# Readout matrices beside the injection, late modulation and scan at fewer steps a chunk

## Chip, core and metric

One core of a Trainium2 chip runs the whole program. The time is device time in microseconds from one launch to its end; the median of several runs is given, and one run more is recorded by the hardware profiler. Five engines work from queues of their own, each strictly in its queue's order: TensorE (PE; its weight loads are shown as PEld), VectorE (DVE), ScalarE (ACT), GpSimd (POOL) and SyncE (SP, which here only issues DMA transfers).

## What is computed

One layer of a generator for 512 latent tokens of width 2048 and 256 context tokens. Cut to the parts that the change touches:

```python
mod_lat = jax.nn.silu(c) @ w_mod[l] + b_mod[l]
sh1, sc1, g1, sh2, sc2, g2 = jnp.split(mod_lat[:, None, :], N_MOD, axis=-1)
h = modulate(x, norm1_w[l], sh1, sc1)
z = h @ w_in[l]
y_a = s5_branch(z[..., :S5_WIDTH], ...)      # bidirectional diagonal state space, 64 groups
y_b = pool_branch(z[..., S5_WIDTH:S5_WIDTH + POOL_WIDTH], ...)
x = x + g1 * merge_branches(z, y_a, y_b, proj_a[l], proj_b[l], w_out[l])
x = x + g2 * peer_ffn(modulate(x, norm2_w[l], sh2, sc2), ...)
# merge_branches: (sigmoid(gate_a) * (y_a @ proj_a) + sigmoid(gate_b) * (y_b @ proj_b)) @ w_out
```

## The kernel before

Everything is float32. A product takes three matmuls: high half by high half, high by low, low by high. `wload` brings a weight chunk of 512 KB to `wraw` by SP, ScalarE copies its high half `whi` (L125), and VectorE (in the expert stage also GpSimd) subtracts for the low half `wlo` (L126). A chunk feeds 24 matmuls of 512 columns in the stages before the experts.

The stages in the order of the program: modulation and normalisation; the state space's input `zs` (`psz`); the pooling inputs and four blocks of the first gate (`psz`, then `psg`), beside which the injection runs; the window products with the matrix `wm` (`psp`, L732) and the pooling products (`psy`); the gates with the projection `proj_b` (`psg`, `psp`, eight blocks of six chunks, then four of four); the readout of the state space (`psr`); the merge (`w_glu`, `proj_a`); the output projection `w_out` (`pso`); then the experts, about two thirds of the time.

Small work that no big product needs at once runs in *lanes*: generators, of which `tick`, called once for each weight chunk, takes a number of steps given by the lane's rate. In this kernel:

- `s5_inject` (rate 2.5) turns `zs` through the loaded matrices `m1` into the states' inputs `B` (`psb`, L663); its loads and stores are issued by GpSimd.
- `s5_scan` (rate 4) runs the recurrence over `B` on VectorE, four operations a step (L678 to L681), 94 steps and 8 steps of reordering.
- `s5_toeplitz` and `s5_m3` (rate 0.7) make the readout's matrices. The first adds two diagonals (`gdiag`) and stores them eight times into `td`, and copies the rest in DRAM. The second makes 32 groups of six GpSimd operations each (L616 to L621) in the tile `m3`, of which there is one, and stores each group to `m3d` by SP (L622). The next group's first write to `m3` (L616) waits until the store is done.
- `mod_late` (rate 3.4) makes the last four quarters of the modulation, each in four blocks of 512 columns. A step loads 256 KB of `w_mod` (`lw`, by SP) and accumulates on VectorE (`lacc`, L819); after the 16 steps of a block one TensorE product sums over the partitions (`psl`, L824), VectorE adds the bias (`lrow`), and GpSimd stores the row to `modd`.

The tile framework gives each tile buffers of its pool, reuses the space of a closed pool, adds the waits that follow from both, and sets each engine's order by a timeline of its own; `high_priority` moves instructions ahead in it. So the order in the code isn't that of the queues. The tiles of the pool `zp` (`wm` and the window products) and of the scan take space that the injection's pools have left.

## Time and profile before

| | us |
|---|---|
| three runs, median (lowest, highest) | 3934.92 (3920.32, 3938.32) |
| profiled execution, device time | 3923.52 |
| its span, first to last instruction | 3921.8 |
| TensorE busy, VectorE busy | 3686.4, 2732.1 |
| GpSimd busy, ScalarE busy | 1834.7, 1178.3 |

In the profile, "busy" of TensorE holds matmuls that overlap in the pipeline: one of 0.39 us is followed by the next after 0.23. A table of stages shows busy times in stretches that I chose by the first and last rows of each stage. A list of waits says which engine's line sat idle for which other, in total, how often, and at most. In the list of single instructions, the bracket at the end of a row is idle time ahead of it and what ended that. SPq is SP's queue; a duration there is that of the issue, and a transfer lands later.

### The profile page before, as it was taken

To read this page: it belongs to the slowest core of one execution; us is meant where nothing else is said; L and a number is where in the kernel's file an instruction comes from. 1 tells how busy PE (TensorE), PEld (TensorE's weight loads), DVE (VectorE), ACT (ScalarE), POOL (GpSimd) and SP (SyncE) were. 2 spreads that over 40 slices of the span, in tenths; PEclk is the share of its full clock that TensorE was granted. 3 is DMA by queue.
4 is the path that set the end of the run, shared out by engine and by line. 5 is a ranking of instruction groups with operands and counts; after the bars stand their busy time and mean duration, and the time that the engine had idled before them with its cause. 6 is when DMAs were issued, how large, how long until landed. Compare 5 with 4: busy or idle time off the path is not lost. (4 is left out here: it accounts for less than half of the span.)

```text
span 3921.8 us, 49308 instructions
## 1 busy us (share of the span) xinstructions
PE 3686.4 (94%) x18841; PEld 3128.2 (80%) x18841; DVE 2732.1 (70%) x3331; ACT 1178.3 (30%) x1752; POOL 1834.7 (47%) x997
## 2 busy tenths in 40 slices
PE   5999998879899989899999999999999999999997
PEld 2478876657777868799999999999877878878886
DVE  4364369997473268999999999965666665666564
ACT  3223331112232232233333333333332333333232
POOL 0043115553223223355555655555565776676652
PEclk8999999999999999999999999999999999999999
DMA  8635658879876422378878878788887988888773
GB/s 263 213 118 182 213 165 231 225 218 289 245 235 199 135 75 91 105 248 285 299 282 300 301 286 300 278 300 296 320 301 258 321 298 286 304 298 298 273 278 120
DMA packets 456381, 954.40 MB, mean 243 GB/s; under 512 B 104720, under 2 KB 248464, under 8 KB 421072
## 3 DMA queue, kind: packets, MB, share of 16 engines
q1 hardware_dynamic: 380320, 584.58, 46.6%
q0 software_dynamic: 46464, 301.03, 21.0%
q10 hardware_dynamic: 29360, 65.64, 4.5%
q8 instruction: 147, 2.41, 0.2%
q14 instruction: 90, 0.74, 0.1%
HBM read 859.88 MB, written 94.93 MB: 243 GB/s over the span
## 5 line engine op out<-in xcount | busy, mean ns | idle before, releaser
L125 ACT CAST whi<-wraw 128x1024 fp32r<-128x1024 f32 x712 | 746.4, 1050 | 1724.9 <-PE psU L111 307.3
L126 POOL TENSOR_TENSOR wlo<-wraw,whi 128x1024 fp32r<-128x1024 f32 x284 | 792.5, 2791 | 803.6 <-ACT whi L125 591.6
L126 DVE TENSOR_TENSOR wlo<-wraw,whi 128x1024 fp32r<-128x1024 f32 x428 | 621.2, 1451 | 560.1 <-ACT whi L125 309.4
L112 PE MATMUL psU<-h2Th,wlo 128*128 128x384 f32 x2048 | 696.8, 340 | 42.5 <-DVE wlo L126 26.0
L110 PE MATMUL psU<-h2Th,whi 128*128 128x384 f32 x2048 | 702.0, 343 | 5.2 <-ACT whi L125 5.1
L111 PE MATMUL psU<-h2Tl,whi 128*128 128x384 f32 x2048 | 694.3, 339 | 0.0
L111 PE MATMUL psV<-wlo,ah 128*128 128x512 f32 x1536 | 607.0, 395 | 12.9 <-POOL wlo L126 7.1
L112 PE MATMUL psV<-whi,al 128*128 128x512 f32 x1536 | 605.9, 394 | 0.0
L110 PE MATMUL psV<-whi,ah 128*128 128x512 f32 x1536 | 556.1, 395 | 4.3 <-DVE ffn L1231 4.3
L112 PEld LDWEIGHTS psU<-h2Th,wlo 128*128 128x128 f32 x2048 | 388.8, 190 | 50.9 <-DVE wlo L126 19.3
L1096 DVE SCALAR_TENSOR_TENSOR row<-row,h 128x2048 f32<-128x2048 f32 x128 | 352.3, 2752 | 81.8 <-DMA row<-in_u,eid 81.7
L110 PEld LDWEIGHTS psU<-h2Th,whi 128*128 128x128 f32 x2048 | 388.6, 190 | 7.3 <-ACT whi L125 7.1
L111 PEld LDWEIGHTS psU<-h2Tl,whi 128*128 128x128 f32 x2048 | 389.0, 190 | 0.0
L1089 DVE SCALAR_TENSOR_TENSOR ffn<-row,w,ffn 128x2048 f32<-128x2048 f32 x127 | 351.3, 2766 | 18.0 <-DMA row<-in_v,eid 17.9
L111 PEld LDWEIGHTS psV<-wlo,ah 128*128 128x128 f32 x1536 | 290.1, 189 | 85.5 <-POOL wlo L126 11.7
L1081 POOL DMA_INDIRECT row<-in_u,eid x128 | 221.4, 1730 | 269.4 <-ACT w L1097 132.5
L110 PEld LDWEIGHTS psV<-whi,ah 128*128 128x128 f32 x1536 | 289.7, 189 | 71.1 <-issue 4.7
L112 PEld LDWEIGHTS psV<-whi,al 128*128 128x128 f32 x1536 | 289.5, 189 | 67.0
L1081 POOL DMA_INDIRECT row<-in_v,eid x128 | 277.0, 2164 | 20.0 <-issue 9.2
L819 DVE SCALAR_TENSOR_TENSOR lacc<-lw,sil,lacc 128x512 f32<-128x512 f32 x240 | 213.7, 891 | 58.6 <-DMA lw<-in_w_mod 56.5
L112 PE MATMUL psg<-hhi,wlo 128*128 128x512 f32 x512 | 203.1, 401 | 25.9 <-DVE wlo L126 25.8
L1144 DVE TENSOR_TENSOR oh<-io,iT 128x512 bf16<-128x512 bf16 x192 | 211.6, 1141 | 6.3 <-PE psd L1152 6.2
(349 smaller groups left out, 5567.4 us busy)
## 6 DMA issues: line engine op xcount, KB each, us to landing
wraw<-in_uT SPq DMA_DIRECT2D x256, 512.0 KB
wraw<-in_v SPq DMA_DIRECT2D x256, 512.0 KB
lw<-in_w_mod SPq DMA_DIRECT2D x256, 256.0 KB
wraw<-in_w_in SPq DMA_DIRECT2D x96, 512.0 KB
wmod<-in_w_mod SPq DMA_DIRECT2D x48, 512.0 KB
sd<-sev ACTq DMA_DIRECT2D x64, 384.0 KB
gds<-ast ACTq DMA_DIRECT2D x12, 2048.0 KB
sr<-sd SPq DMA_DIRECT2D x32, 768.0 KB
```

Source lines behind the costliest of these rows:

```text
L110: mm(ps, a.hi, b.hi, start=start, stop=False)
L111: mm(ps, a.hi, b.lo, start=False, stop=False)
L112: mm(ps, a.lo, b.hi, start=False, stop=stop)
L125: nc.scalar.copy(hi, raw)
L126: ins = (eng or nc.vector).tensor_tensor(lo, raw, hi.bitcast(F32), op=OP.subtract)
L819: nc.vector.scalar_tensor_tensor(acc, w, self.sil[:, k, 0:1], acc, op0=OP.mult, op1=OP.add)
L1081: nc.gpsimd.indirect_dma_start(out=r, out_offset=None, in_=I[tab], in_offset=bass.IndirectOffsetOnAxis(ap=eid[:, k:k + 1], axis=0))
L1089: V.scalar_tensor_tensor(acc, v, w, acc, op0=OP.mult, op1=OP.add)
L1096: V.scalar_tensor_tensor(u, u, 1.0, h2, op0=OP.mult, op1=OP.mult, accum_out=w[:, 0:1])
L1144: V.tensor_tensor(oh[:, q], self.io4, iT[:, q, ts].unsqueeze(2).broadcast_to([P, NT, P]), op=OP.is_equal)
```

## The change

The two generators of readout matrices become one lane of rate 1.3, the matrices first, which starts with the injection and is emptied before the window products; both use the one pool `m3`, the diagonals in four rounds of 256 columns, in the tile of the matrices, in place of two of 512. `par2` is loaded for eight groups of the state space at a time in place of four. The injection's `m1` comes in halves of 256 KB, in buffers of half the size. The scan's lane goes from 4 to 2 steps a chunk. The late modulation's goes from 3.4 to 2.4, holds three of the four quarters, has two accumulators, and sums a block six steps into the next one; the last quarter becomes a second lane (rate 1.3) beside merge and output projection, with a pool of its own on the left side of SBUF. The readout ticks the lanes twice in each of its eight blocks.

The diff, cut:

```diff
@@ -192,6 +192,8 @@
         self.tail()
+        self.drain(self.lane_g2)
+        self.es_g2.close()
         self.peer()
...
@@ -374,22 +376,26 @@
         s5 = self.es()
+        es_m3 = self.es()
+        lane_m = self.lane(1.3, [self.s5_m3(es_m3), self.s5_toeplitz(es_m3)])
         lane_i = self.lane(2.5, [self.s5_inject(s5)])
...
         with self.es() as s6:
-            yb, lane_s = self.pool_branch(s6, es_b, hlat, s5, lane_i)
-            lane_m = self.lane(0.7, [self.s5_toeplitz(), self.s5_m3()])
-            lane = self.lane(3.4, [self.mod_late()])
+            yb, lane_s = self.pool_branch(s6, es_b, hlat, s5, lane_i, lane_m, es_m3)
+            lane = self.lane(2.4, [self.mod_late("late", "right", ((0, 2), (2, 4), (1, 3)))])
             self.gates(hlat, yb)
         es_h.close()
         self.drain(lane_s)
-        self.drain(lane_m)
         self.check("gates")
+        self.es_g2 = self.es()
+        late2 = self.mod_late("late2", "left", ((3, 5),))
+        next(late2)
         with self.es() as s7:
             gt = self.s5_readout(s7)
             self.drain(lane)
             es_b.close()
+            self.lane_g2 = self.lane(1.3, [late2])
             es_m = self.es()
             m = self.merge(s7, es_m, gt)
         self.m, self.es_m = m, es_m
...
-    def s5_toeplitz(self):
...
-        with self.es() as es:
-            sp = es.enter_context(self.tc.tile_pool(name="toep", bufs=1, side="right"))
-            for hf in range(2):
-                cs = slice(hf * 512, hf * 512 + 512)
-                gf = sp.tile([H, 2, 512], F32, tag="gdiag", name=self.nm("gdiag"))
-                nc.sync.dma_start(gf[:, 0], self.gd[112:128, 0, cs])
-                nc.sync.dma_start(gf[:, 1], self.gd[0:16, 1, cs])
-                nc.gpsimd.tensor_tensor(gf[:, 0], gf[:, 0], gf[:, 1], op=OP.add)
-                for t in range(Q):
-                    nc.sync.dma_start(self.td[t * H:(t + 1) * H, t, cs], gf[:, 0])
...
+    def s5_toeplitz(self, es):
+
+        nc, sp = self.nc, self.m3p
+        for q4 in range(4):
+            cs = slice(q4 * 256, q4 * 256 + 256)
+            gf = sp.tile([H, 2, 256], F32, tag="m3", name=self.nm("gdiag"))
+            nc.sync.dma_start(gf[:, 0], self.gd[112:128, 0, cs])
+            nc.sync.dma_start(gf[:, 1], self.gd[0:16, 1, cs])
+            nc.gpsimd.tensor_tensor(gf[:, 0], gf[:, 0], gf[:, 1], op=OP.add)
             for t in range(Q):
+                nc.sync.dma_start(self.td[t * H:(t + 1) * H, t, cs], gf[:, 0])
+            yield
+        for t in range(Q):
+            if t:
+                nc.sync.dma_start(self.td[0:t * H, t, :], self.gd[(Q - 1 - t) * H:(Q - 1) * H, 0, :])
...
+            if t % 2:
+                yield
...
-    def s5_m3(self):
+    def s5_m3(self, es):
...
-        with self.es() as es:
-            sp = es.enter_context(self.tc.tile_pool(name="m3", bufs=1, side="right"))
+        sp = self.m3p = es.enter_context(self.tc.tile_pool(name="m3", bufs=1, side="right"))
+        if True:
...
-                if gq * GM % 4 == 0:
-                    par = sp.tile([P, 2, H, 4], F32, tag="par2", name=self.nm("par2"))
-                    nc.sync.dma_start(par, self.I["s5bc"][gq * GM // GB][:, 2:4, :, gq * GM % GB:gq * GM % GB + 4])
...
+                if gq * GM % GB == 0:
+                    par = sp.tile([P, 2, H, GB], F32, tag="par2", name=self.nm("par2"))
+                    nc.sync.dma_start(par, self.I["s5bc"][gq * GM // GB][:, 2:4])
...
@@ -652,15 +658,15 @@
-                m1 = mp.tile([P, 4, 2, P], F32, tag="m1", name=self.nm("m1"))
-                nc.gpsimd.dma_start(m1.rearrange("p g r d -> p (g r d)"), self.m1d[gb, :, g4 * 1024:(g4 + 1) * 1024])
-                if g4 == 0 and i + 1 < NGB:
-                    nxt = chunks(order[i + 1])
                 for g2 in range(2):
+                    m1 = mp.tile([P, 2, 2, P], F32, tag="m1", name=self.nm("m1"))
+                    nc.gpsimd.dma_start(m1.rearrange("p g r d -> p (g r d)"), self.m1d[gb, :, g4 * 1024 + g2 * 512:g4 * 1024 + g2 * 512 + 512])
+                    if g4 == 0 and g2 == 0 and i + 1 < NGB:
+                        nxt = chunks(order[i + 1])
                     ps = self.psT.tile([P, 512], F32, tag="tr", name=self.nm("psb"))
...
@@ -691,7 +697,7 @@
-    def pool_branch(self, es, es_b, hlat, s5, lane_i):
+    def pool_branch(self, es, es_b, hlat, s5, lane_i, lane_m, es_m3):
...
@@ -718,8 +724,10 @@
             self.drain(lane_i)
             s5.close()
+            self.drain(lane_m)
+            es_m3.close()
             self.scp = es_b.enter_context(pool(name="scan", bufs=2, side="right"))
-            lane_s = self.lane(4, [self.s5_scan()])
+            lane_s = self.lane(2, [self.s5_scan()])
...
@@ -801,16 +809,32 @@
-    def mod_late(self):
...
-        nc, es = self.nc, self.es()
-        lp = es.enter_context(self.tc.tile_pool(name="late", bufs=4, side="right"))
+    def mod_late(self, name, side, parts):
...
+        nc = self.nc
+        es = self.es() if side == "right" else self.es_g2
+        lp = es.enter_context(self.tc.tile_pool(name=name, bufs=4 if side == "right" else 2, side=side))
-        for q, blk in ((0, 2), (2, 4), (1, 3), (3, 5)):
+        pend = None
+
+        def close(acc, q, n, c0):
+            row = lp.tile([1, N], F32, tag="lrow", name=self.nm("lrow"), bufs=1)
+            nc.gpsimd.dma_start(row, self.I["b_mod"][0:1, c0:c0 + N])
+            ps = self.psT.tile([P, 512], F32, tag="tr", name=self.nm("psl"))
+            nc.tensor.matmul(ps[0:1, :], self.ones[:, 0:1], acc, start=True, stop=True)
+            nc.vector.tensor_tensor(row, row, ps[0:1, :], op=OP.add)
+            nc.gpsimd.dma_start(self.modd[:, q * D + n * N:q * D + (n + 1) * N], row)
+
+        if side == "left":
+            yield
+        for q, blk in parts:
             for n in range(D // N):
                 c0 = blk * D + n * N
-                acc = lp.tile([P, N], F32, tag="lacc", name=self.nm("lacc"), bufs=1)
+                acc = lp.tile([P, N], F32, tag="lacc", name=self.nm("lacc"), bufs=2)
                 for k in range(KT):
+                    if k == 6 and pend is not None:
+                        close(*pend)
+                        pend = None
                     w = lp.tile([P, N], F32, tag="lw", name=self.nm("lw"))
...
                     yield
-                row = lp.tile([1, 2, N], F32, tag="lrow", name=self.nm("lrow"), bufs=1)
-                nc.gpsimd.dma_start(row[:, 1], self.I["b_mod"][0:1, c0:c0 + N])
-                ps = self.psT.tile([P, 512], F32, tag="tr", name=self.nm("psl"))
-                nc.tensor.matmul(ps[0:1, :], self.ones[:, 0:1], acc, start=True, stop=True)
-                nc.vector.tensor_tensor(row[:, 0], row[:, 1], ps[0:1, :], op=OP.add)
-                nc.gpsimd.dma_start(self.modd[:, q * D + n * N:q * D + (n + 1) * N], row[:, 0])
-                yield
-        es.close()
+                pend = acc, q, n, c0
+        for _ in range(6):
+            yield
+        close(*pend)
+        yield
+        if side == "right":
+            es.close()
...
@@ -860,6 +883,8 @@
                     nc.sync.dma_start(dsk, I["s5_d"][0:1, ch].broadcast_to([NCL, P]))
+                self.tick()
+                self.tick()
```

What that does to the queues, at three places. The first is GpSimd's queue where the four early gate blocks end (`sad` are their stores, `m` with 128x1024 or 128x512 the injection's loads, the other `m` and `m3t` a group of readout matrices). Before:

```order
L656 DMA m_535_3291<-m1d 128x1024
L656 DMA m_541_3339<-m1d 128x1024
L781 DMA sad<-sg_3984 128x512
L781 DMA sad<-sg_3987 128x512
L822 DMA lrow_4611<-in_b_mod 1x16x32
L584 TENSOR_TENSOR gdiag_4275<-gdiag_4275 16x512
L584 TENSOR_TENSOR gdiag_4287<-gdiag_4287 16x512
L608 TENSOR_SCALAR npar_4384<-par_698_4382 128x64
L616 TENSOR_TENSOR m_700_4386<-pm_4380,par_698_4382 128x256
L617 TENSOR_TENSOR m3t_4387<-pm_4380,par_698_4382 128x256
```

and now:

```order
L622 TENSOR_TENSOR m_594_3517<-pm_3051,par_556_3298 128x256
L625 TENSOR_TENSOR m_594_3517<-pm_3051,npar_3300 128x256
L789 DMA sad<-sg_4409 128x512
L624 TENSOR_TENSOR m_594_3517<-m_594_3517,m3t_3518 128x256
L789 DMA sad<-sg_4412 128x512
L663 DMA m_571_3380<-m1d 128x512
L663 DMA m_578_3408<-m1d 128x512
L626 TENSOR_TENSOR m3t_3518<-pm_3051,par_556_3298 128x256
L652 DMA ud<-U_3386 128x8x64
L627 TENSOR_TENSOR m_594_3517<-m_594_3517,m3t_3518 128x256
L663 DMA m_585_3457<-m1d 128x512
L614 TENSOR_SCALAR npar_3580<-par_604_3578 128x128
```

The last two `sad` stores stood behind every load of the injection, with the groups behind them and beside the gates; now they stand in the sixteenth of the 32 groups (tiles `m_419` to `m_688` in the order of the rows), and eight loads of the injection are still behind them.

The second is SP's queue around the load of `wm`. Before:

```order
L741 DMA wraw_4116<-in_pool_w 128x2x256
L741 DMA wraw_4144<-in_pool_w 128x2x256
L124 DMA wraw_4175<-in_w_in 128x4x256
L726 DMA wm<-in_wm 128x512
L124 DMA wraw_4242<-in_w_in 128x4x256
L124 DMA wraw_4347<-in_w_in 128x4x256
L124 DMA wraw_4431<-in_w_in 128x4x256
L815 DMA lw_4209<-in_w_mod 128x512
```

and now:

```order
L628 DMA m3d<-m_688_4096 128x512
L586 DMA gdiag_4135<-gd 16x256
L587 DMA gdiag_4135<-gd 16x256
L590 DMA td<-gdiag_4135 16x256 x8
L586 DMA gdiag_4177<-gd 16x256
...
L590 DMA td<-gdiag_4231 16x256 x8
L734 DMA wm<-in_wm 128x512
L124 DMA wraw_4653<-in_w_in 128x4x256
...
L839 DMA lw_4623<-in_w_mod 128x512
```

The load of `wm` followed the pooling weights and the next gate chunk; now it follows the last `m3d` stores and the four rounds of diagonals, and the gates' next weight chunks and the late modulation's first loads follow it. TensorE's first product with `wm` is row 1539 of its order before and now, right behind the last product of the injection.

The third is SP's queue at the readout's first loads (`rU`, `rT`, `rm`, `rd`). Before:

```order
L854 DMA rU_7944<-ud 128x512
L622 DMA m3d<-m_1273_6948 128x512
L815 DMA lw_7248<-in_w_mod 128x512
L856 DMA rT_7946<-td 128x8x128
L858 DMA rm_1451_7948<-m3d 128x4x512
L124 DMA wraw_7413<-in_w_in 128x4x256
L815 DMA lw_7251<-in_w_mod 128x512
L862 DMA rd_7952<-in_s_d 64x128
L854 DMA rU_7996<-ud 128x512
```

and now:

```order
L124 DMA wraw_8527<-in_w_glu 128x4x256
L839 DMA lw_8366<-in_w_mod 128x512
...
L877 DMA rU_7790<-ud 128x512
L879 DMA rT_7792<-td 128x8x128
L881 DMA rm_1392_7794<-m3d 128x4x512
L885 DMA rd_7798<-in_s_d 64x128
L877 DMA rU_7857<-ud 128x512
...
L885 DMA rd_7865<-in_s_d 64x128
L839 DMA lw_8146<-in_w_mod 128x512
```

The first two sets stood among weight chunks of the gates; now they stand behind all of these and behind the first chunks of `w_glu`, with accumulation loads ahead of them and after them. On VectorE 171 accumulation steps stand between the first and the last low half of the gates, before 199; 42 stand beside the readout's first products, before 10.

## Rows read from the trace of the kernel before

**Rows 1.** Table of stages.

```profile
core 0: us, PE busy (x) PEld busy (x) DVE busy (x) ACT busy (x) POOL busy (x), PEclk, DMA share, GB/s
378.00:527.40 149.40, 146.13 (x811) 125.35 (x809) 49.06 (x69) 53.09 (x115) 26.90 (x40) 1.00 0.65 200
527.40:989.00 461.60, 406.30 (x1672) 311.65 (x1672) 406.83 (x702) 95.92 (x115) 205.09 (x257) 0.96 0.81 234
989.00:1063.00 74.00, 60.25 (x461) 55.65 (x461) 25.49 (x34) 14.28 (x18) 20.06 (x11) 0.91 0.88 242
1063.00:1200.00 137.00, 132.29 (x569) 103.88 (x568) 99.67 (x119) 43.31 (x56) 43.61 (x29) 1.00 0.73 233
1200.00:1384.00 184.00, 180.56 (x773) 144.87 (x771) 58.86 (x59) 46.32 (x65) 49.65 (x45) 1.00 0.48 158
```

**Rows 2.** Single TensorE instructions: start us, us, engine, line, tiles, how many, idle before.

```profile
527.38 7.38 PE L732 MATMUL psp<-wm,us 128*128 128x128 f32 x64 [2.96 <-DMA wm<-in_wm]
...
549.16 0.39 PE L110 MATMUL psg<-hhi,whi 128*128 128x512 f32 x1
...
551.20 0.39 PE L110 MATMUL psg<-hhi,whi 128*128 128x512 f32 x1
...
980.62 1.02 PE L824 MATMUL psl<-lacc,ones 128*1 128x512 f32 x2
```

**Rows 3.** Waits of TensorE in the gates: us in total, times, longest.

```profile
PE psg L112 <- DVE wlo L126: 25.8, 15, 5.6
PE psp L112 <- DVE wlo L126: 22.1, 10, 4.0
PE psl L824 <- DVE lacc L819: 7.2, 4, 3.3
```

**Rows 4.** VectorE's groups in the gates (busy us, mean ns), then ns min/median/max of two.

```profile
L819 DVE SCALAR_TENSOR_TENSOR lacc<-lw,sil,lacc 128x512 f32<-128x512 f32 x185 | 166.4, 899 | 41.3 <-DMA lw<-in_w_mod 40.1
L126 DVE TENSOR_TENSOR wlo<-wraw,whi 128x1024 fp32r<-128x1024 f32 x65 | 84.1, 1295 | 5.5 <-ACT whi L125 4.8 <-PE psg L112 0.6
L678 DVE TENSOR_TENSOR sa<-ar,B 128x128 f32<-128x128 f32 x92 | 39.9, 434 | 1.1
...
L678 DVE TENSOR_TENSOR sa<-ar,B x94: 271/292/2406, 525.3 to 876.7; 128x128 f32<-128x128 f32 x94
...
L819 DVE SCALAR_TENSOR_TENSOR lacc<-lw,sil,lacc x240: 732/752/2549, 552.1 to 1142.6; 128x512 f32<-128x512 f32 x120
```

**Rows 5.** Single GpSimd instructions, end of preparation and last gate store.

```profile
378.15 0.86 POOL L636 DMA_DIRECT2D R<-zs  x1 [18.48 <-PE pg L563]
...
521.58 0.55 POOL L781 DMA_DIRECT2D sad<-sg  x1 [0.46 <-ACT sg L780]
```

**Rows 6.** Single GpSimd instructions, one diagonal round and a matrix group.

```profile
566.61 1.79 POOL L584 TENSOR_TENSOR gdiag<-gdiag 16x512 f32<-16x512 f32 x1 [9.65 <-DMA lw<-in_w_mod]
...
690.59 0.62 POOL L616 TENSOR_TENSOR m<-pm,par 128x256 f32<-128x256 f32 x1
...
693.62 0.72 POOL L621 TENSOR_TENSOR m<-m,m3t 128x256 f32<-128x256 f32 x1
...
698.61 0.78 POOL L616 TENSOR_TENSOR m<-pm,par 128x256 f32<-128x256 f32 x1 [3.23 <-DMA m3d<-m]
```

**Rows 7.** Single issues in SP's queue: start us, us, line, transfer, how many.

```profile
524.49 0.34 SPq L726 DMA_DIRECT2D wm<-in_wm  x1
...
557.84 3.28 SPq L586 DMA_DIRECT2D td<-gdiag  x7
...
562.70 0.32 SPq L582 DMA_DIRECT2D gdiag<-gd  x1
...
695.34 0.38 SPq L622 DMA_DIRECT2D m3d<-m  x1
```

**Rows 8.** Table of stages, the fullest slice for DMA.

```profile
900.00:950.00 50.00, 45.81 (x197) 36.65 (x198) 35.25 (x42) 10.39 (x12) 19.23 (x26) 1.00 0.99 315
```

**Rows 9.** Readout's first loads: ns min/median/max, first and last start us.

```profile
L854 SPq DMA_DIRECT2D rU<-ud x8: 326/357/576, 898.7 to 1043.4; - x8
```

More of the change, by code (lines that the diff above doesn't have):

```diff
@@ L573, in s5_prep @@
             yield
[L574 to L594 removed]
+    def s5_toeplitz(self, es):
[6 more added lines that the diff above has]
+            nc.gpsimd.tensor_tensor(gf[:, 0], gf[:, 0], gf[:, 1], op=OP.add)
+            for t in range(Q):
+                nc.sync.dma_start(self.td[t * H:(t + 1) * H, t, cs], gf[:, 0])
[3 more added lines that the diff above has]
+                nc.sync.dma_start(self.td[0:t * H, t, :], self.gd[(Q - 1 - t) * H:(Q - 1) * H, 0, :])
+            if t < Q - 1:
+                nc.sync.dma_start(self.td[(t + 1) * H:P, t, :], self.gd[H:(Q - t) * H, 1, :])
+            if t % 2:
+                yield
+    def s5_m3(self, es):
         nc, Gp = self.nc, self.nc.gpsimd
         GM = 2
[L598 to L599 removed]
+        sp = self.m3p = es.enter_context(self.tc.tile_pool(name="m3", bufs=1, side="right"))
+        if True:
             for gq in range(G // GM):
@@ L603, in s5_m3 @@
                     nc.sync.dma_start(pm, self.pmd[gq * GM // 16])
-                if gq * GM % 4 == 0:
-                    par = sp.tile([P, 2, H, 4], F32, tag="par2", name=self.nm("par2"))
-                    nc.sync.dma_start(par, self.I["s5bc"][gq * GM // GB][:, 2:4, :, gq * GM % GB:gq * GM % GB + 4])
-                    npar = sp.tile([P, H, 4], F32, tag="npar", name=self.nm("npar"))
+                if gq * GM % GB == 0:
+                    par = sp.tile([P, 2, H, GB], F32, tag="par2", name=self.nm("par2"))
+                    nc.sync.dma_start(par, self.I["s5bc"][gq * GM // GB][:, 2:4])
+                    npar = sp.tile([P, H, GB], F32, tag="npar", name=self.nm("npar"))
                     Gp.tensor_scalar(npar, par[:, 0], -1.0, None, op0=OP.mult)
                 shp = [P, Q, H, GM]
-                gl = slice(gq * GM % 4, gq * GM % 4 + GM)
+                gl = slice(gq * GM % GB, gq * GM % GB + GM)
                 gp = slice(gq * GM % 16, gq * GM % 16 + GM)
@@ L662, in s5_inject @@
                         for ri in range(2):
-                            nc.tensor.matmul(ps[:, (2 * j + ri) * NCH:(2 * j + ri + 1) * NCH], m1[:, g2 * 2 + j, ri, :],
+                            nc.tensor.matmul(ps[:, (2 * j + ri) * NCH:(2 * j + ri + 1) * NCH], m1[:, j, ri, :],
                                              U[:, g4 * 4 + g2 * 2 + j, :], start=True, stop=True)
```

6 lines of the change are left out of this document (removed).

## The prediction, made before the changed kernel was run

> **What bounds the kernel now.** I read the table of stages first, then the waits, then single rows. In the table [rows 1] the injection (378 to 527.4) leaves TensorE no gap: it is busy 146.1 of 149.4 us, while GpSimd has 26.9 us of work. The gates (527.4 to 989) are the stage that loses time: VectorE is busy 406.8 of 461.6 us. What TensorE has to do there is countable: 64 weight chunks (8 x (4 + 2) + 4 x 4) of 24 matmuls are 1536 matmuls, and an undisturbed one starts 0.227 us after the other (nine steps in 2.04 us [rows 2]), so 348 us; 48 more for the pooling products are 11, the window products 7.4, and twelve modulation sums of 1.0 us are 12 [rows 2]. That is a floor of 378 us, and 461.6 - 378 = 84 us are lost. The waits say to whom: to VectorE's low halves of the weights, 25.8 and 22.1 us, and to the modulation's accumulator, 7.2 us [rows 3].
>
> VectorE's groups in that stage say why [rows 4]: 185 accumulation steps of 899 ns (and 41 us of waiting, nearly all for their weights), 65 low halves, and 92 scan steps of four operations. The durations are swollen: the accumulation's median is 752 ns, the first scan operation's 292 against a mean of 434, with single ones up to 2406 ns. In the same stretch GpSimd is busy 205 us [rows 1], most of it with the 32 readout-matrix groups.
>
> **The change, part by part.**
>
> *(a) Readout matrices beside the injection: a wait of TensorE.* In GpSimd's new order the 32 groups of six operations stand between the injection's loads; the last pair of `sad` stores of the four early gate blocks stands within the 16th group, so 16 whole groups are behind it. On SP's queue the load of `wm` stands behind all 32 `m3d` stores and four diagonal rounds, and in TensorE's order the first product with `wm` has the same 1539 rows ahead of it as before. Engines take their rows in order, so TensorE can do nothing else in that time, and the scan, the gates' weight loads and the late modulation wait behind the same load. When `wm` lands is the sum of a chain:
>
> - The groups can't start before 378.15, where GpSimd leaves the preparation [rows 5]. The last `sad` issue is at 521.58 in the trace [rows 5] and waits for TensorE's gate blocks. The first 16 groups need 8.2 to 9.5 us each: 7.2 from below, plus `par` loads and 0.55 to 0.9 us for each DMA issue in between, of which there are 16 more because `m1` comes in halves. 16 x 9 from 382 is 526. I take 530, with 518 (no delay of the gate blocks) and 560 (the queues hold one another up) as bounds.
> - A group lasts from one L616 to the next: 690.59 to 698.61, 8.0 us [rows 6]. In it five operations end at 694.34; SP issues the store at 695.34 [rows 7], a microsecond late because it was busy with other loads; and the buffer, of which there is one, is free at 698.61, 3.3 us after the issue. Without the delay it is 7.0. I take 7.2 (6.9 to 8.0): 16 x 7.2 = 115 us, and 5 us for the rest of the 16th group and its store.
> - Four loads of `par` must land before their `npar`: some 1.5 us each beyond the store's wait, 6 us (4 to 12), estimated from the 3.3 us of a store.
> - A diagonal round: load at 562.70 [rows 7], its add at 566.61 [rows 6], 3.9 us; an add of half the size, 1 us (1.8 for the full one); eight stores of 0.47, 3.8 us (seven in 3.28 [rows 7]); the buffer back at most 1.6 us later (the first round's stores end at 561.12, the next load is at 562.70). That is 10 us, and there are four in place of two, one after the other because they share the matrices' one buffer: 40 us (38 to 46).
> - `wm` itself: issue at 524.49 [rows 7], first product at 527.38 [rows 2], 3 us.
>
> Sum: 530 + 5 + 115 + 6 + 40 + 3 = 699, against 527.4 before: **+172 us**, with 151 and 227 from the bounds. It can't come out below zero: 16 groups at the 4.4 us that six operations alone take (3.75 and one more of 0.62 [rows 6]) put the landing past 620.
>
> *(b) The gates without the groups, and slower lanes.* By the order 171 accumulation steps lie in the gates, before 199. VectorE loses 28 x 0.9 = 25 us of them; if the rest falls to the medians, 25 more there, some 38 in the scan (145 us for the four operations to 93 x 1.15) and 5 in the low halves. 407 becomes about 315, below TensorE's floor, and all 84 lost microseconds could come back. I take **-50** (20 to 85): in the new order the steps come in bunches, four to six of them in 32 of the 64 chunks and none in 24. A chunk with five and one scan step is 1.2 + 5 x 0.75 + 1.15 = 6.1 us of VectorE against 5.45 of TensorE, and it loads 5 x 256 + 512 KB, 330 GB/s, more than the 315 of the fullest stretch here [rows 8]. The wait of 7.2 us for the accumulator goes: there are two now, and the sum is put off by six steps.
>
> The Trainium skill, "SBUF — State Buffer", section "Who interferes with whom", says that a VectorE instruction with two SBUF inputs and a GpSimd instruction that reads SBUF shut each other out for a whole instruction. The trace agrees in direction (single operations of 2406 ns against a median of 292 [rows 4]); the page says nothing of the loads. By it alone the gates would fall to their floor, which is rival 5.
>
> *(c) The readout starts later.* Before, its first loads go out from 898.7 [rows 9], 90 us ahead of the first product. Now they stand behind the last gate chunk, their tiles wait for the last gate's `sad` store, and 42 accumulation steps stand among the readout's VectorE work in place of 10. Exposed: some 5 us for the store (3.3 for an `m3d` store, with its issue and the sigmoid ahead of it) and 7 for a set of 2 MB at 290 GB/s; then 32 x 256 KB = 8 MB more are 28 us, of which the stretch has room for about half (it moves 242 GB/s now [rows 1]). 12 + 14 = 26; I take **+22** (8 to 35).
>
> *(d) At nothing:* the last quarter's 64 steps (48 us at the median) beside merge and output projection, where VectorE is busy 99.7 of 137 and 58.9 of 184 us [rows 1]. If that cover failed, TensorE, idle 4.7 and 3.4 us there, would lose some 10 us. The quarter's `modd` stores on GpSimd hold `x1d` stores back by a few microseconds, and nobody waits for those. The scan at two steps a chunk takes 51 of 64 chunks and ends some 70 us before the readout.
>
> **Sum:** 172 - 50 + 22 = +144. The profiled execution took 3923.5 us (span 3921.8), near the fastest of the three runs shown (3920.3 to 3938.3, median 3934.9). 3923.5 + 144 = 4067.5, so **4068 us**.
>
> **The rivals.**
> 1. *The matrices do fit beside the injection* (faster). Then (a) is zero: 3923.5 - 50 + 22 = 3896, or 3861 with 85 from the gates. For it: GpSimd is idle over 120 us there. Against it: 32 groups and four rounds would have to be done in 149 us, 3.4 us a group, and six operations alone take 4.4. That figure decides it.
> 2. *A short wait, and gates at their floor.* The stores come back as fast as the diagonal's, 1.6 us, so a group is 5.4, and the early half keeps pace (518): 518 + 4 + 16 x 5.4 + 4 + 36 + 3 = 651, +124; with -85 and +8 the time is 3970. Against it: the store of the matrices at 698.61, with 3.3 us.
> 3. *The queues hold one another up.* GpSimd's next group waits for a store; SP issues it behind a weight load, which waits for VectorE and so for TensorE, which waits for an injection load behind the group on GpSimd. At the upper bounds (a) is +227, and with -35 and +22 the time is 4137. For it: SP's microsecond of delay. Against it: only the injection's loads tie TensorE to this circle.
> 4. *The change doesn't do what it says:* the gates stay bound by loads and bunches, -5: 3923.5 + 172 - 5 + 22 = 4112.
> 5. *The gates fall to their floor.* With the groups gone every VectorE operation takes its median, 315 us in all, and the loads keep up with the bunches: 3923.5 + 172 - 85 + 22 = 4032. For it: the swollen means; against it: the 330 GB/s of a bunch.
>
> [...]
>
> **Chances and range.** Forecast 0.57, rival 1 0.03, rival 2 0.10, rival 3 0.12, rival 4 0.06, rival 5 0.12. The range goes from 3995, which leaves out rivals 1 and 2, to 4135, which takes in rivals 4 and 5 and about half of rival 3. A measurement of this kernel can tell about 0.5% (20 us) from no change: faster 0.03, within 0.02 (the lower end of rival 2), slower 0.95.
>
> **What would show it.** Right: TensorE idle in one piece of 150 to 200 us that ends with the first `wm` product near 700, its wait put down to the load of `wm`; GpSimd's groups about 7.2 us apart in it; from there to the readout some 410 us; scan operations near 290 ns. Wrong: `wm` at 560 or earlier, groups closer than 5 us, or gates as long as 455 us.

## The result, and the profile after

The changed kernel takes 4025.7 us (median of four runs, 4021.95 to 4036.49) against 3928.0 before: a ratio of 1.0242, 95% interval 1.0213 to 1.0270. It is slower by 98 us where +144 was forecast; the profiled execution's span went from 3921.8 to 4020.2. The table of stages of the kernel after (columns as in [rows 1]; the stretches again by the first and last rows of each stage):

```profile
core 0: us, PE busy (x) PEld busy (x) DVE busy (x) ACT busy (x) POOL busy (x), PEclk, DMA share, GB/s
374.00:545.00 171.00, 158.18 (x807) 134.95 (x805) 51.31 (x61) 52.05 (x113) 119.14 (x171) 0.91 0.67 207
545.00:658.70 113.70, 0.00 (x0) 0.03 (x1) 3.54 (x14) 0.54 (x2) 57.64 (x90) 0.50 0.14 45
658.70:1044.00 385.30, 380.69 (x1666) 306.12 (x1666) 309.49 (x665) 95.40 (x114) 22.16 (x41) 0.99 0.69 222
1044.00:1063.30 19.30, 0.29 (x3) 0.07 (x2) 8.45 (x12) 2.91 (x4) 1.62 (x3) 0.63 1.05 328
...
1138.00:1288.00 150.00, 141.75 (x630) 113.77 (x629) 95.14 (x108) 45.36 (x57) 43.95 (x27) 0.98 0.66 205
```

The second row is new: 113.7 us in which TensorE does nothing, VectorE next to nothing, and GpSimd half of the time. The third is the gates, 461.6 us in [rows 1] and 385.3 now, with TensorE busy nearly throughout. The fourth is a hole of 19 us ahead of the readout, with the DMA engines full. The waits of TensorE (us in total, times, longest) name all three, the first three lines from the gates with the stretch ahead of them, the last two from the readout:

```profile
PE psp L740 <- DMA wm<-in_wm: 114.0, 1, 114.0
PE psg L112 <- DVE wlo L126: 2.9, 2, 1.6
PE psp L112 <- DVE wlo L126: 1.7, 2, 1.3
...
PE psr L896 <- DMA rT<-td: 22.7, 4, 19.0
PE psr L897 <- DMA rm<-m3d: 7.4, 4, 3.8
```

The 25.8 and 22.1 us of [rows 3] have become 2.9 and 1.7. VectorE's groups in the gates (busy us, mean ns of one, idle ahead), which answer [rows 4]:

```profile
L843 DVE SCALAR_TENSOR_TENSOR lacc<-lw,sil,lacc 128x512 f32<-128x512 f32 x158 | 118.1, 748 | 35.6 <-DMA lw<-in_w_mod 34.7
L126 DVE TENSOR_TENSOR wlo<-wraw,whi 128x1024 fp32r<-128x1024 f32 x65 | 79.2, 1220 | 26.7 <-PE psg L112 16.7 <-issue 7.2 <-PE psp L112 2.4
L684 DVE TENSOR_TENSOR sa<-ar,B 128x128 f32<-128x128 f32 x91 | 26.2, 288 | 1.5
```

The accumulation's mean is 748 ns (899 before), the scan's first operation 288 (434): both are at the median of before.

A ledger of both profiled executions, by the first and last TensorE rows of each stage:

| us | before | after | difference | forecast |
|---|---|---|---|---|
| start of the program to first `wm` product | 527.4 | 658.7 | +131.3 | +172 |
| to the last gate product | 461.3 | 385.2 | -76.1 | -50 |
| to the first readout product | 0.4 | 19.4 | +19.0 | +22 for these two |
| to the first product of the output projection | 211.8 | 224.8 | +13.0 | |
| to the experts (first `psU`) | 392.4 | 399.9 | +7.5 | 0 |
| experts | 2328.5 | 2332.2 | +3.7 | 0 |

### The profile page after: what moved, and what is told of

Read it like the earlier page. It is cut to its first block, busy times and chain, and to the rows that moved or that the text cites. A ratio compares the mean times of both kernels' runs of the same rounds, so it can differ in the third digit from the quotient of the medians.

```text
span 4020.2 us, 49345 instructions
## 1 busy us (share of the span) xinstructions
PE 3689.3 (92%) x18841; PEld 3141.6 (78%) x18841; DVE 2677.5 (67%) x3331; ACT 1175.9 (29%) x1752; POOL 1809.7 (45%) x1007
## 5 line engine op out<-in xcount | busy, mean ns | idle before, releaser
L126 DVE TENSOR_TENSOR wlo<-wraw,whi 128x1024 fp32r<-128x1024 f32 x428 | 610.0, 1426 | 548.4 <-ACT whi L125 283.1
L843 DVE SCALAR_TENSOR_TENSOR lacc<-lw,sil,lacc 128x512 f32<-128x512 f32 x240 | 199.2, 831 | 96.8 <-DMA lw<-in_w_mod 95.0
L1169 DVE TENSOR_TENSOR oh<-io,iT 128x512 bf16<-128x512 bf16 x192 | 220.9, 1190 | 9.7 <-PE psd L1177 9.7
L1171 DVE TENSOR_TENSOR R<-oh,wb 128x1536 bf16<-128x1536 bf16 x96 | 203.0, 2115 | 1.7
```

What stands on the lines that cost most here:

```text
L126: ins = (eng or nc.vector).tensor_tensor(lo, raw, hi.bitcast(F32), op=OP.subtract)
L843: nc.vector.scalar_tensor_tensor(acc, w, self.sil[:, k, 0:1], acc, op0=OP.mult, op1=OP.add)
L1169: V.tensor_tensor(oh[:, q], self.io4, iT[:, q, ts].unsqueeze(2).broadcast_to([P, NT, P]), op=OP.is_equal)
L1171: V.tensor_tensor(R, oh[:, 1].unsqueeze(1).broadcast_to([P, 3, NT, P]), wb[:, :, ts].unsqueeze(3).broadcast_to([P, 3, NT, P]), op=OP.mult)
```

## Experiments

The theory is that these are separate effects: the emptying of the matrices' lane costs the wait for `wm`; the missing groups, through GpSimd's operations, give the gates' gain; and the second late pool and the slower lanes cost the readout. The rivals put the gates' gain down to the slower lanes or to less traffic, and the readout's loss to its loads' place in the queue. All times below are medians, and each ratio is to the kernel before as run beside it; stages come from the profiled executions, of which there is one for each kernel, and they scatter: with the same code ahead of `wm`, its first product came between 653.3 and 661.9 us in the changed kernel and experiments 2, 4 and 5, and the experts, which no edit touches, took 2325.8 to 2338.2 us.

**1. The slower lanes alone.** The matrices stay beside the gates:

```diff
-        lane_m = self.lane(1.3, [self.s5_m3(es_m3), self.s5_toeplitz(es_m3)])
...
+            lane_m = self.lane(0.7, [self.s5_toeplitz(), self.s5_m3()])
             lane = self.lane(2.4, [self.mod_late("late", "right", ((0, 2), (2, 4), (1, 3)))])
```

> The changed kernel with the readout matrices back beside the gates, in pools of their own at 0.7 steps a chunk as before; everything else of the change stays (scan at 2, late modulation at 2.4 with the fourth quarter later, halves of m1, ticks in the readout). Theory: the wait for wm is gone (first wm product near 527), the stage from there to the last gate product takes about 440 us (461.6 before, 385 after), since VectorE has 27 accumulation steps fewer but GpSimd's groups still swell its operations (scan operations near 430 ns); the readout still starts about 19 us after the last gate product, and 22 to 32 us are lost there. Time 3923 - 20 + 28, about 3930. Rival A, the gates' gain of the change is all from the slower lanes: 390 us in the gates, scan operations near 290 ns, time near 3880. Rival B, it is all from the missing groups: 460 us, time near 3950.

3975.7 us, ratio 1.0095 (1.0059 to 1.0131). The gates take 453.7 us, only 8 less than before, and the readout begins 21.2 us late and takes 225.0. VectorE's and GpSimd's groups in the gates:

```profile
L841 DVE SCALAR_TENSOR_TENSOR lacc<-lw,sil,lacc 128x512 f32<-128x512 f32 x158 | 137.4, 869 | 37.2 <-DMA lw<-in_w_mod 35.7
L684 DVE TENSOR_TENSOR sa<-ar,B 128x128 f32<-128x128 f32 x92 | 38.1, 414 | 1.6
L627 POOL TENSOR_TENSOR m<-m,m3t 128x256 f32<-128x256 f32 x32 | 27.4, 855 | 2.1
```

With as few steps as in the kernel after, the means are nearly those of [rows 4]. The theory expected 20 us from the lanes; it is 8, nearer to rival B's nothing. Rival A falls. The first `wm` product came at 538.95, 12 us later than before, which nothing in the theory provided for (experiment 9). The time is 45 us above the 3930 expected: besides these 12 and the 12 missing in the gates, the hole and the readout cost 34 us in place of 28, and the stages from the output projection on are 14 longer than before.

**2. The matrices alone**, old lanes and old late modulation:

```diff
-            lane = self.lane(2.4, [self.mod_late("late", "right", ((0, 2), (2, 4), (1, 3)))])
+            lane = self.lane(3.4, [self.mod_late()])
...
-            lane_s = self.lane(2, [self.s5_scan()])
+            lane_s = self.lane(4, [self.s5_scan()])
...
```

> The kernel before with only the matrices moved beside the injection and emptied before the window products (and m1 in halves); scan at 4, late modulation at 3.4 steps with all four quarters, no ticks in the readout, no second late pool. Theory: the wait for wm is the same as in the changed kernel (first wm product near 659, +131), the gates take about 395 us because VectorE's operations fall to their medians (scan near 290 ns, accumulation near 750 ns), and the readout's first loads go out ahead of the last gates, so nothing is lost there: 3923 + 131 - 66 = 3988. Rival A (the slower lanes made the gates' gain): gates 455 us, time near 4048. Rival C (the readout's loss comes from the matrices' move): 19 us of gap here too, time near 4015.

3981.1 us, ratio 1.0133 (1.0099 to 1.0167). First `wm` product at 657.2, gates 391.0 us, no hole, readout to output projection 204.0 us. VectorE's groups in the gates, with more accumulation steps than before [rows 4], and means at the medians of before:

```profile
L821 DVE SCALAR_TENSOR_TENSOR lacc<-lw,sil,lacc 128x512 f32<-128x512 f32 x193 | 143.8, 745 | 47.1 <-DMA lw<-in_w_mod 45.7
L678 DVE TENSOR_TENSOR sa<-ar,B 128x128 f32<-128x128 f32 x91 | 25.9, 285 | 1.3
```

Rivals A and C fall. So of the gates' 76 us the move of the matrices brings 70 and the lanes 6 to 8, and the readout's loss belongs to the lanes and the late pools. The two runs add up to the changed kernel: +52 and +56 us of span are +108; the 12 us by which `wm` is late in experiment 1 (experiment 9) lie under the wait in the changed kernel, which leaves 96 against the +98.4 measured.

**3. The matrices' operations left out** of the kernel before, in the gates, with their loads and stores kept:

```diff
-                Gp.tensor_tensor(m3[:, 0], er, c_, op=OP.mult)
...
-                Gp.tensor_tensor(m3[:, 1], m3[:, 1], tmp, op=OP.subtract)
+                if gq == 0:
+                    m3 = sp.tile([P, 2, Q, H, GM], F32, tag="m3", name=self.nm("m3"))
+                    Gp.memset(m3, 0.0)
```

> The kernel before without the six GpSimd operations of each readout-matrix group (one cleared tile is stored 32 times in their place, so the matrices are zero); the loads for them and the stores of 8 MB stay. Theory: in the gates it is GpSimd's operations that swell VectorE's, so these fall to their shortest (scan 285 ns, accumulation 750 ns) and the stage takes 391 to 396 us as where the groups lay elsewhere: time about 3857. Rival F, it is the traffic of the matrices and VectorE's own amount of work: gates 440 us or more, time 3900 or more.

3888.3 us (two runs), ratio 0.9902 (0.9867 to 0.9937). One cleared tile is stored 32 times in place of the groups. VectorE's operations in the gates fell to what experiment 2 shows, as expected:

```profile
L814 DVE SCALAR_TENSOR_TENSOR lacc<-lw,sil,lacc 128x512 f32<-128x512 f32 x171 | 128.4, 751 | 67.0 <-DMA lw<-in_w_mod 65.1
L673 DVE TENSOR_TENSOR sa<-ar,B 128x128 f32<-128x128 f32 x92 | 26.4, 287 | 1.8
```

But the gates took 408.9 us, not 391 to 396 (and not rival F's 440). GpSimd's operations account for 52 of the 70 us, or somewhat less, since 16 accumulation steps fewer than before lay in the gates here; in what remains VectorE waits 65 us for `lw`, 46 in experiment 2, so the stores and loads beside the gates are the likeliest cause of the other 18. That they are was not tried by itself. The readout stretch was 222.4 us, with 73 accumulation steps in it (58 before); why more of them came to lie there was not followed up.

**4. The readout's tiles back in their place.** The second late pool takes 10 KB below them:

```diff
-            s.enter_context(pool(name="pad", bufs=1)).tile([P, 4096], F32, name="pad")
+            s.enter_context(pool(name="pad", bufs=1)).tile([P, 1536], F32, name="pad")
```

> The changed kernel with the readout's unused tile `pad` cut from 4096 to 1536 columns, that is by the 10 KB that the second late pool takes below it, so that the readout's tiles lie where they lay in the kernel before. Theory: the readout's first loads waited for space of the last gates, moved under them by those 10 KB; now they go out some 80 us ahead of the last gate product, the 19.3 us gap before the first readout product falls to under 3, and the stretch from the last gate product to the output projection loses 20 to 30 us: time 3995 to 4003. Rival D, the gap comes from the accumulation loads and the weight chunks that stand ahead of the readout's loads, and the readout's slower course from its 42 accumulation steps: gap 15 us or more, time 4015 to 4025.

4010.9 us, ratio 1.0193 (1.0167 to 1.0218). The first `rU` goes out at 956.5, 91 us ahead of the first readout product (in the kernel after at 1057.6, and 898.7 in [rows 9]); the hole is 0.4 us. SP's issues of `rU`, with ns of the shortest, median and longest, and first and last start:

```profile
L877 SPq DMA_DIRECT2D rU<-ud x8: 326/327/692, 956.5 to 1111.5; - x8
```

Rival D falls for the hole: 10 KB of address, not the queue, moved the loads. Its other half, that the accumulation steps slow the readout, is taken up in experiment 5; the time lies between theory and rival. The stretch behind the hole grew from 224.8 to 231.1, so 13 us of 19 remained as gain (15 by the medians of the two kernels). The table of stages, readout and merge, shows where the rest is. Here:

```profile
1047.50:1136.10 88.60, 68.59 (x470) 61.19 (x470) 55.27 (x64) 15.26 (x18) 22.43 (x15) 0.85 1.01 281
1136.10:1278.60 142.50, 131.05 (x565) 103.20 (x564) 91.69 (x105) 43.63 (x56) 39.81 (x25) 1.00 0.69 213
```

And the same two stages in experiment 2:

```profile
1048.50:1115.90 67.40, 56.87 (x460) 52.70 (x459) 18.40 (x26) 14.28 (x18) 19.98 (x10) 0.95 0.90 235
1115.90:1252.50 136.60, 133.26 (x576) 104.92 (x575) 100.30 (x121) 44.14 (x56) 43.87 (x29) 1.00 0.74 236
```

The readout itself takes 88.6 us in place of 67.4: 64 VectorE operations in place of 26, of which 38 are accumulation steps in place of 2, and the DMA engines full (1.01).

**5. The three quarters done within the gates**, on top of experiment 4:

```diff
-            lane = self.lane(2.4, [self.mod_late("late", "right", ((0, 2), (2, 4), (1, 3)))])
+            lane = self.lane(3.4, [self.mod_late("late", "right", ((0, 2), (2, 4), (1, 3)))])
...
-                self.tick()
-                self.tick()
```

> The changed kernel with pad at 1536 columns, the late modulation's three quarters at 3.4 steps a chunk in place of 2.4, and no ticks in the readout, so that its 192 steps end within the gates; the fourth quarter stays beside merge and output projection. Theory: the gates take 386 to 392 us, since VectorE has room there, and the stretch from the first readout product to the output projection falls from 231 to 205 to 212 us, as its accumulation steps and their loads are gone: time 3985 to 3995. Rival H, the fourth quarter's lane beside the merge makes the stretch longer: 222 us or more, time 4000 or more.

4004.5 us, ratio 1.0205 (1.0177 to 1.0233). The stretch is 216.3 us, between theory and rival H. Its two parts, readout and merge, answer separately (table of stages):

```profile
1051.90:1122.50 70.60, 61.96 (x467) 57.99 (x466) 36.58 (x39) 15.30 (x19) 20.49 (x11) 0.90 0.95 267
1122.50:1268.20 145.70, 134.25 (x565) 105.31 (x564) 105.00 (x121) 43.48 (x56) 41.40 (x26) 0.98 0.73 232
```

Waits in the merge, TensorE's and VectorE's, here:

```profile
PE psp L112 <- DVE wlo L126: 11.0, 8, 2.3
DVE lacc L843 <- DMA lw<-in_w_mod: 31.3, 18, 3.6
```

and in experiment 2:

```profile
PE psp L112 <- DVE wlo L126: 2.1, 2, 1.1
DVE lacc L821 <- DMA lw<-in_w_mod: 8.1, 9, 2.1
```

The readout is back at 70.6 us with 16 accumulation steps beside it in place of 38, so 22 steps had cost 18 us. The merge takes 9 us more than in experiment 2, and TensorE waits there 11.0 us for low halves. The number of steps isn't the reason, which is 49 here and 48 there. What differs is the fourth quarter's lane, whose loads come late: VectorE stands 31.3 us ahead of a step for want of `lw`, and low halves queue behind. The lane's pool has two buffers for `lw` in place of four; that this is why was not tried. The gates took 398.3 us against 386 to 392 expected, and 7 more than in experiment 2, although that has the faster scan lane; this stays unexplained, and a gain on experiment 4 is not shown (ratios 1.0205 and 1.0193).

**6. The diagonals beside the gates**, all 32 groups beside the injection, pad at 1536:

```diff
-        lane_m = self.lane(1.3, [self.s5_m3(es_m3), self.s5_toeplitz(es_m3)])
+        lane_m = self.lane(1.3, [self.s5_m3(es_m3, 0, 32)])
...
+            lane_m = self.lane(0.7, [self.s5_toeplitz()])
```

> The changed kernel with pad at 1536 columns, all 32 matrix groups beside the injection and emptied before the window products, but the diagonals beside the gates, in two rounds as before. Theory: each piece of work behind the last gate store has its price in TensorE's wait, 8.0 us a diagonal round, so the first wm product comes 32 us earlier than with the rounds, near 629; the rounds hide beside the gates (387 to 392 us there): time 3976 to 3986. Rival G, the wait is mostly the space that wm takes over and not the sum of what is left: first wm product at 645 or later, time 3995 or more.

3981.1 us, ratio 1.0136 (1.0109 to 1.0163). The first `wm` product came at 627.75, 34 us earlier than in experiment 4, for four rounds of 8.0 us, and rival G falls; the wait is a sum of what is left in the lane. The gates took 393.1 us, 8 more than in experiment 4, so the rounds didn't quite hide there.

**7. Half of the groups**: 16 beside the injection, 16 and the diagonals beside the gates, the slower lanes kept, pad at 1536:

```diff
-        lane_m = self.lane(1.3, [self.s5_m3(es_m3), self.s5_toeplitz(es_m3)])
+        lane_m = self.lane(1.3, [self.s5_m3(es_m3, 0, 16)])
...
+            lane_m = self.lane(0.7, [self.s5_toeplitz(), self.s5_m3(es_m4, 16, G // 2)])
```

> The changed kernel with only the first 16 matrix groups beside the injection; the other 16 and the diagonal rounds (two of 512 columns, as before) go beside the gates at 0.7 steps a chunk in pools of their own; and pad at 1536 columns. Theory: TensorE waits for wm for under 15 us (first product 527 to 545), the gates take 395 to 420 us with half of the groups in them, the readout's loads go out early: 3923 + 8 - 55 + 8, about 3885, less than both kernels. Rival E, the emptying of the lane as such costs, however few groups are left, since wm and the scan take the space of the injection's last loads: first wm product near 570, time near 3925.

3928.2 us, ratio 1.0001 (0.9982 to 1.0021). The long wait is gone (3.1 us for `wm`), so rival E falls, but the first `wm` product comes at 547.4, just past what was expected. The gates take 422.6 us and the readout stretch 231.1, which eats the gain: 43 us above the 3885 expected, rival E's time without its mechanism.

**8. Half of the groups, everything else as in the kernel before** but for the injection's loads in halves; against experiment 7, cut:

```diff
             lane_m = self.lane(0.7, [self.s5_toeplitz(), self.s5_m3(es_m4, 16, G // 2)])
-            lane = self.lane(2.4, [self.mod_late("late", "right", ((0, 2), (2, 4), (1, 3)))])
+            lane = self.lane(3.4, [self.mod_late()])
...
```

> The kernel before with only half of the matrices moved: 16 groups beside the injection (m1 in halves), the other 16 and the diagonals beside the gates at 0.7 steps a chunk; scan and late modulation at the old rates, no second late pool, no ticks in the readout. Theory, by the pieces measured: first wm product at 546 (+19), gates 391 + 16 x 2.2 = 426 (-35), no gap, readout stretch 206 (-6), the rest as before (+3): 3923 - 19 = 3904, 0.5% faster than before. Rival I, the late modulation's steps and the groups collide in the gates again: 440 us there, time 3918, no difference.

3906.7 us, ratio 0.9950 (0.9933 to 0.9968): faster than both kernels, and by what the pieces gave. First `wm` product at 542.5, gates 429.4 (so rival I's 440 falls), no hole, readout stretch 208.1.

**9. The injection's loads in halves**, the only edit to the kernel before (`m1` as in the change):

> The kernel before with one edit: the injection's loads m1 come in halves of 256 KB, in two buffers of half the size. Theory: with half the data in flight, the last blocks of the injection, which run alone once the gate blocks are done, wait for each load; the first wm product comes at 539 in place of 527 (the 12 us that show where the matrices stay beside the gates and the halves are the only edit ahead of wm), and the time is 3937. Rival J, the halves cost nothing, and it was the late pools or the lanes that moved wm: 527, time 3926.

3938.1 us, ratio 1.0029 (1.0015 to 1.0043). The first `wm` product came at 543.15, 16 us late (12 in experiment 1), so rival J falls. The profiled execution took 3950.1 us, among the slowest of the ten runs; by the medians the halves cost 11 us. The table of stages ahead of `wm`, with the `wm` products as its last row:

```profile
378.00:519.50 141.50, 139.12 (x747) 118.45 (x745) 43.04 (x53) 49.03 (x100) 32.45 (x50) 1.00 0.62 193
519.50:543.20 23.70, 15.30 (x65) 13.63 (x65) 6.26 (x15) 4.31 (x16) 3.23 (x6) 0.54 0.31 108
543.20:553.20 10.00, 10.00 (x65) 10.00 (x66) 8.15 (x24) 4.10 (x7) 0.00 (x0) 0.72 0.01 2
```

Single products of the injection's end, with the idle time ahead of each:

```profile
525.21 1.99 PE L663 MATMUL psb<-U,m 128*128 128x96 f32 x8 [0.55 <-DMA m<-m1d]
527.84 1.99 PE L663 MATMUL psb<-U,m 128*128 128x96 f32 x8 [0.64 <-DVE B L667]
```

And one in the kernel before:

```profile
514.93 1.92 PE L663 MATMUL psb<-U,m 128*128 128x96 f32 x16
```

Eight products take 1.99 us where sixteen took 1.92. Of the injection's 256 products 80 come behind the last gate block here, 32 in the kernel before. There TensorE waits for its loads and for VectorE, the granted clock falls to 0.54, and the last blocks run at half speed. Why the loads in halves leave more of the injection for the end, the smaller transfers or the smaller space, was not tried apart.

**10. The injection's loads from SP's queue**, on top of experiment 8 (`nc.gpsimd.dma_start(m1...)` becomes `nc.sync.dma_start`):

> The split of 16 and 16 groups with the old lanes (split16_old), and the injection's m1 loads issued by SP in place of GpSimd. Theory: GpSimd's queue, which holds 32 issues of 0.55 us and the groups, was what delayed the loads; first wm product near 532 (542.5 with GpSimd's issues), gates 429 as there, time 3897. Rival K, a load of m1 that waits for its buffer in SP's queue holds the gate blocks' weight chunks behind it: first wm product at 545 or later, time 3910 or more.

3899.9 us, ratio 0.9920 (0.9903 to 0.9938). First `wm` product at 540.3: neither 532 nor 545. GpSimd's queue was not what delayed the injection's end. The gain on experiment 8 is 7 us by the medians, and the intervals touch; it is the fastest kernel here that leaves no work out, but that it beats experiment 8 is not shown.

**11 and 12. Twelve and twenty groups** in place of sixteen:

> As split16_old with 12 groups beside the injection and 20 beside the gates. Theory: a group costs 2.2 to 2.4 us beside the gates and at most 0.5 beside the injection: first wm product 541, gates 438, time 3914. Rival L, the groups beside the injection delay it as much as they save later: first wm product 535 or less, time 3905 or less.

> As split16_old with 20 groups beside the injection and 12 beside the gates. Theory: four groups lie behind the last gate store, and at 5.5 us each they pass the injection's own end by some 10 us: first wm product 552, gates 420, time 3906. Rival M, the four groups still fit beside the injection's last blocks: first wm product 544, gates 420, time 3898.

3915.3 us (ratio 0.9970, 0.9956 to 0.9984) and 3919.2 us (0.9977, 0.9957 to 0.9996). The first `wm` products with 12, 16 and 20 groups:

```profile
546.68 9.52 PE L738 MATMUL psp<-wm,us 128*128 128x128 f32 x64 [3.06 <-DMA wm<-in_wm]
542.53 10.31 PE L738 MATMUL psp<-wm,us 128*128 128x128 f32 x64 [3.29 <-DMA wm<-in_wm]
559.82 9.20 PE L738 MATMUL psp<-wm,us 128*128 128x128 f32 x64 [17.05 <-issue]
```

Twelve: first `wm` product at 546.7, gates 436.3, as expected but for the 6 us in the injection. Twenty: 559.8 and 417.3. The four groups behind the last gate store cost more than was expected, 17.3 us against 542.5, 4.3 each, so the point where the groups stop being free for `wm` lies between 16 and 20. Rivals L and M fall with these. Of the whole time the intervals of 12, 16 and 20 groups overlap, so that 16 is the best number is not shown. With the old lanes the gates take 461.3, 436.3, 429.4, 417.3 and 391.0 us with 32, 20, 16, 12 and no groups: 2.2 to 2.4 us for each group beyond none. The kernel with none has no diagonals beside the gates either; but from 12 to 32 groups, all with diagonals there, it is 2.2 as well.

## Why the prediction was right or wrong

**(a) The wait for `wm`: right in place and mechanism, 41 us too long** (+131 for +172). The chain is the one that was worked out, and its terms were mis-sized:

- *The last early gate store*: forecast at 530, measured 519.5 (-10), near the bound of 518. The groups beside the injection kept pace at 9.2 us each, for 9 in the sum; GpSimd started them at 376 in place of 382.
- *A group* (-22 with the rest of the 16th): 7.2 us forecast, 5.5 measured, 6.0 where `par` is loaded. Single GpSimd instructions of the wait:

```profile
584.54 0.63 POOL L622 TENSOR_TENSOR m<-pm,par 128x256 f32<-128x256 f32 x1 [1.38 <-DMA m3d<-m]
585.13 0.63 POOL L625 TENSOR_TENSOR m<-pm,npar 128x256 f32<-128x256 f32 x1
585.72 0.72 POOL L624 TENSOR_TENSOR m<-m,m3t 128x256 f32<-128x256 f32 x1
586.52 0.63 POOL L626 TENSOR_TENSOR m3t<-pm,par 128x256 f32<-128x256 f32 x1
587.23 0.72 POOL L627 TENSOR_TENSOR m<-m,m3t 128x256 f32<-128x256 f32 x1
588.03 0.63 POOL L623 TENSOR_TENSOR m3t<-pm,par 128x256 f32<-128x256 f32 x1
590.03 0.63 POOL L622 TENSOR_TENSOR m<-pm,par 128x256 f32<-128x256 f32 x1 [1.37 <-DMA m3d<-m]
```

  The idle time for the store is 1.4 us (3.23 in [rows 6]), and one operation of the next group, the first into `m3t`, runs under it. The store's 3.3 us had been read in a stretch that moved 234 GB/s; in the wait the kernel moves 45. That the traffic is the reason fits, but was not tried by itself. From the last gate store to the end of the last `m3d` store it took 104 us (519.5 to 623.5), 126 in the sum; the first of the 16 groups still took 9.0, among the injection's loads.
- *The rounds*: adds at 625.66, 633.61, 641.71 and 649.56, 8.0 us apart in place of 10 (-8 in all): from the issue of the load at 623.49 to the add it is 2.2 us here, 3.9 in the row that the term was taken from.

Rival 2 had named exactly this, a store that returns in 1.6 us and 5.4 us a group; it was set aside on a row from the loaded gates. Its +124 for (a) was nearer to the measured +131 than the forecast. SP issued the last `m3d` store at 621.49 and the load that waits for its buffer at 623.49, 2.0 us later. The Trainium skill, "DMA: Bandwidth & Descriptors", section "Anatomy of one DMA", fits 2.0 us and the bytes at 436 GB/s to transfers that GpSimd issues, an estimate by that page of 2.6 us for 256 KB; SP issues these stores, and the measurement is below that.

**(b) The gates: right sign, too cautious** (-76 for -50). The swollen VectorE operations took their medians, and TensorE was busy 380.7 of 385.3 us; that is nearly rival 5. The step that failed is the choice of -50 because of the bunches: the stage moved 222 GB/s, no slice of 20 us more than 287, and TensorE waited 4.6 us in all for low halves. Of the two reasons given for the gain, the matrices' absence brings 70 us (experiment 2) and the 28 steps fewer, 25 us of VectorE's time, only 6 to 8 of the stage (experiments 1 and 2). The Trainium skill, "SBUF — State Buffer", section "Who interferes with whom", whose rule of mutual exclusion stood beside rival 5, is borne out by experiment 3 as far as durations go (434 to 287 ns); the 18 us that stayed lost there are waiting and not durations.

**(c) The readout: right size for half a reason** (+32 for +22). The hole was forecast as 12 and measured as 19. The prediction saw that the tiles wait for the last gate's store; that 10 KB of the second late pool were the cause it did not say (experiment 4). The steps beside the readout were forecast as 14 us for their loads; with 38, 16 and 2 of them it takes 88.6, 70.6 and 67.4 us (experiments 4, 5 and 2). In the changed kernel, 29 of the steps lie beside the readout and 10 in the hole ahead of it.

**(d) "At nothing": nearly.** The merge takes 138.5 to 145.8 us in the six kernels with the lane of the fourth quarter and 136.6 to 139.7 in the eight without it, 5 us more on average (9 in experiment 5); from the output projection to the experts it is 395.0 to 399.9 and 392.3 to 396.4, 3 us more. That is close to the 10 that were given for a failed cover. The halves of `m1` the prediction counted only as issues; they make `wm` 12 to 16 us late where nothing else does (experiments 1 and 9), hidden in the changed kernel, where `wm` comes later than the injection's end anyway.

The whole came out 42 us below the 4068 forecast. Parts (a) and (b) erred by 41 and 26 us to the same side; (c) and the stages behind it cost 10 and 11 us more than forecast and gave back a third. In (a) and (b) the kernel behaves as rival 2 says, whose 3970 the stated range left out: (a) +131 where rival 2 has +124, (b) -76 where it has -85. What brought the time into the range is the readout, +32 where rival 2 has +8, with a cause that was only half foreseen, and the 11 us counted as nothing. So the sign and the chain were foreseen, but that the number fell into the range is in part luck.

The signs named beforehand say the same: the one piece of idle time was 114 us long and not 150 to 200, and ended at 658.7 and not near 700; groups were 5.5 us apart and not 7.2; the 404 us from there to the readout and the scan's 288 ns were as forecast, and no sign of being wrong appeared. Rivals 1 and 3 fell: the matrices don't fit (the sixteen late groups alone took 104 us), and no circle of queues formed, as the early half kept pace. Rival 4 fell with the gates' 385.2 us.

## What to carry to other kernels

Work that hides behind a busy engine is free only up to the point where somebody has to wait for its last piece: move as much of it as ends with its cover, here about 16 of 32 groups, and leave the rest where it was. A duration that holds a DMA's return is best read in a stretch with the traffic of the place that it is moved to. When a pool is opened under others, see which tiles it shifts over space still in use: 10 KB made a hole of 19 us here.

## What the runs showed of the hardware

- A group of six GpSimd operations, with its loads and its store, lengthens by 2.2 to 2.4 us a stage in which TensorE waits for VectorE, whether 12, 16, 20 or 32 groups lie there (with the old lanes); of VectorE's operations the scan's grow from 285 ns to 434, the accumulation's from 745 to 899, the low halves' from 1220 to 1295 (without and with the groups in the gates).
- TensorE's clock: granted 0.50 in the wait of 114 us, that is its level of 1.2 GHz. The first products after it are still slow: single ones of the 64 of `wm` last up to 553 ns with a median of 275, and the 64 take 9.52 us in place of 7.38 [rows 2]:

```profile
658.70 9.52 PE L740 MATMUL psp<-wm,us 128*128 128x128 f32 x64 [114.03 <-DMA wm<-in_wm]
```

- A stretch of small waits had a low clock too: between 519.5 and 543.2 in experiment 9, where TensorE waited 0.55 to 2.9 us ahead of each of the injection's last blocks, the granted clock was 0.54, close to the level of 1.2 GHz; in the stage ahead of it, where it hardly waited, 1.00.
